# Causal masks added by VectorE, and branch gates projected with group 0's values, in a two-layer decoder on one core

## The chip, the cores and the metric

The kernel runs on one core of a Trainium2 chip. A core has TensorE (PE in the rows, with its weight loads as PEld), VectorE (DVE), ScalarE (ACT), GpSimd (POOL) and SyncE (SP), which issues DMAs here. The metric is the device time of one execution in microseconds, as the median of several runs.

## The reference

A sequence of 512 tokens with 1024 numbers each goes through a retention layer and then through a layer of native sparse attention. Cut to what matters here:

```python
def nsa_shared_kv(h, g_kv, w_kv, ...):          # once, keys and values of all branches
    proj = rmsnorm(h, g_kv) @ w_kv
    k_cmp = compress_blocks(kc, pe_k, w1_k, w2_k)      # gelu(blocks @ w1) @ w2
    v_cmp = compress_blocks(vc, pe_v, w1_v, w2_v)
...
def nsa_layer(h, g_norm, w_in, w_out, ...):
    proj = rmsnorm(h, g_norm) @ w_in
    q, gate, bgate = jnp.split(proj, [q_w, q_w + NSA_W], axis=-1)
    gb = jax.nn.sigmoid(bgate)                         # 16 heads x 3 branches
    ...
    valid_w = kwpos[None, :] <= t[:, None]             # causal
    p_w = jax.nn.softmax(jnp.where(valid_w, s_w, NEG), axis=-1)
    ...
    return gates[..., 0:1] * o_c + gates[..., 1:2] * o_s + gates[..., 2:3] * o_w
```

The two gains (g_kv and g_norm) multiply the same normed rows, so both weights can take their gain first and then share the rows. With 512 tokens all selection blocks fall within the 16 that are kept, so the selected branch is a causal softmax like the window branch.

## The kernel before

All products are made of split operands, a high and a low part: `mm3` (lines 347 to 354) issues three matmuls for each pair of chunks, and line 353 is therefore the line of nearly all of TensorE's work. TensorE holds results in PSUM tiles named d, s, pt and o. Weights come through the class `Stream`: blocks of up to 128 x 1024 numbers are loaded, in the order that `order()` writes out by hand, into four raw slots; GpSimd multiplies a gain into a block (line 169), ScalarE rounds it to its high part (line 187), VectorE makes the low part (line 205, and 203 for the gates' block "bg"); six slots hold finished blocks. A call of `tick` in the code puts the next block's steps into the engines' queues at that point, so the order of the code is the order of each engine.

The second layer begins with `norm_rows` (lines 670 to 674) and transposed rows aH, aL; `v_proj` (704 to 714) makes group 0's values for four tiles of tokens from two blocks "kvv" of 256 columns, and the low parts of these blocks are what its matmuls need. `compress` (766 on) then builds compressed keys (b = 0) and values (b = 1). Its `block(s)` adds and splits a block of tokens on VectorE (lines 774, 776 on ScalarE, 779), and then runs 24 matmuls of 256 columns with the weights "wk" or "wv" into tile o; there are eight such steps, and dense products stand between them: for b = 1 the four query products of group 0 (`q_proj`, 24 matmuls of 512 columns, evacuated in line 727). Beside the last part, the gelu with two transposes (line 800), `bg_proj` makes the branch gates: 16 matmuls of 512 columns (lines 865, 866, 868) with weights of 48 or 96 columns, and later four transposes (line 1024) and three small steps (1026 to 1028) bring them to rows. `k_proj` (745 on) follows.

The attention loop runs over 4 groups and 8 units each, a head times two branches. Beside unit u the scores of unit u + 1 are made: `scores` fills three banks s, for token tile 3, tile 2, and tiles 0 and 1; even units carry 32 more columns of compressed keys. After its three products each bank gets the causal mask, as a matmul of the identity `idb` with the triangle `tri` (0 and -1e30, bf16) that adds into the bank: line 927 for tiles 3 and 2, line 941 for both diagonals of the last bank. VectorE then takes negated maxima (line 951), ScalarE exponentials (952), GpSimd scales (965); line 891 adds the mask of the compressed columns. `probs_T` transposes the probabilities in two parts (line 974), and their split (362 on ScalarE, 363 on VectorE) feeds `values`. Dense products (`fillers`) stand before, between and after the parts.

Of the kernel before, what the change touches and what calls it, by code (L numbers as in the profile page):

```python
# [24 lines left out]
M_TRI, M_CMP, M_ID, M_END = 0, 128, 256, 384  # L25
# [22 lines left out]
def order():  # L48
    """The blocks of [128, 1024] that stream in, in the order in which they are used.

    A block is (array, first row, rows, first column, columns)."""
# [41 lines left out]
    o += [("bg", 0, 1024, 0, 48)] + kk(0)  # L93
# [23 lines left out]
class Stream:  # L117
    """Blocks of weights: loaded into raw slots, then multiplied by their gains and split into
    a high and a low part. Every tick moves each of these steps on by a block."""
# [9 lines left out]
    def first(self, n, i):  # L129
        """Splits one half of a block at the start."""  # L130
# [14 lines left out]
    def tick(self, n=None):  # L145
        """Moves on by up to n blocks, as far as there is room."""
# [14 lines left out]
    def mul(self):  # L161
# [4 lines left out]
        if g is not None and w < 512:  # L166
            r3 = raw.rearrange("p (k n) -> p k n", k=m)
            for k in (slice(0, m // 2), slice(m // 2, m)):
                self.nc.gpsimd.tensor_mul(r3[:, k], r3[:, k],  # L169
                                          g[:, k, None].to_broadcast([128, m // 2, w]))  # L170
        self.nm += 1

    def high(self):
# [8 lines left out]
        if self.order[n][0] == "bg":  # L182
            # The low parts go beside the high ones, 48 columns each.
            self.nc.scalar.activation(hi[:, :2 * m * w].rearrange("p (k n) -> p k n", k=m)[:, :, :w],
                                      raw.rearrange("p (k n) -> p k n", k=m), AF.Copy)
        elif g is None or w < 512:
# [7 lines left out]
    def low(self):  # L194
# [6 lines left out]
        if self.order[n][0] == "bg":  # L201
            h, l = (a[:, :2 * m * w].rearrange("p (k n) -> p k n", k=m) for a in (hi, self.hi[s]))
            self.nc.vector.tensor_sub(l[:, :, w:], raw.rearrange("p (k n) -> p k n", k=m), h[:, :, :w])
        elif g is None or w < 512:
# [32 lines left out]
def decoder(ctx: ExitStack, tc: tile.TileContext, x, xT, stream, cst, msk, gains, fnorm, out):  # L237
# [33 lines left out]
    idb = masks[:, M_ID:M_ID + 128]  # L271
# [7 lines left out]
    def scal(n):  # L279
        """Columns for small per-token numbers, handed out in turn."""  # L280
# [10 lines left out]
    def gain(key):  # L291
        n, r0, nr = key[0], key[1], key[2]
        base = {"kv": G_KV, "kvv": G_KV, "nin": G_NSA, "bg": G_NSA, "pg0": G_PLE,
                "pg1": G_PLE + 8, "rout": G_GN}.get(n)
        if base is None:
            return None
        return gn[:, base + r0 // 128:base + (r0 + nr) // 128]
# [3 lines left out]
    # ---- places of layer 1  # L301
# [15 lines left out]
    # ---- constants and the start of the streams  # L317
# [3 lines left out]
    # The clock of the tensor engine rises while the first loads run.  # L321
# [34 lines left out]
    def wst(p, o, k0=0, k1=NK):  # L356
        """Columns of a block on the partitions, tokens along the free axis."""
# [7 lines left out]
    def rstd(ms, scale):  # L365
        """(ms * scale + EPS) ** -0.5 in place."""
# [7 lines left out]
    def to_aT(t, src, bank="pt"):  # L374
        """Rows of tile t onto the free axis, split."""
# [8 lines left out]
    # ---- layer 1: x^T, its reciprocal rms into the rotary tables  # L384
# [319 lines left out]
    def v_proj(g, t, p, bank="d", tick=True):  # L704
# [7 lines left out]
        if t == 3:  # L712
            p[0].done()
            p[1].done()
# [475 lines left out]
```

## Time and profile before

| | |
|---|---|
| median of 3 runs | 1165.9 us (1163.51 to 1167.29) |
| span of the profiled execution | 1164.6 us |
| busy TensorE / weight loads | 1147.4 / 964.1 us |
| busy VectorE / ScalarE / GpSimd | 697.5 / 486.5 / 299.5 us |
| granted TensorE clock over the span | nine tenths or more in each of 40 slices |

The share of busy time is an average over the whole span. TensorE's row is full, so its rare waits show up in the brackets of a timeline's rows, with the engine and the line that ended them, and they are read stage by stage. Matmuls overlap, so the distance from one start to the next tells what one costs, and the duration beside it does not.

### The profile page before, as it was taken

The numbers are of one execution on the slowest core, as the hardware profiler recorded it, in microseconds if no ns is written. First come the engines' busy times: TensorE is split into PE (matmuls) and PEld (weight loads), VectorE is DVE, ScalarE is ACT, GpSimd is POOL, SyncE is SP. The second block draws the span as 40 slices with busy tenths as digits, with TensorE's granted clock in tenths as the row PEclk, the third lists the DMA queues.
The fourth block names the chain that finished last, engine by engine and source line by source line (L and its number), as shares of the span: only waits on it lengthen the run. The fifth ranks groups of instructions, "written<-read, shape, count | busy, mean of one in ns | idle before, by whom it ended". The sixth has DMA issues, their size and how long they took to land. (4 is left out here: it accounts for less than half of the span.)

```text
span 1164.6 us, 15379 instructions
## 1 busy us (share of the span) xinstructions
PE 1147.4 (99%) x5922; PEld 964.1 (83%) x5922; DVE 697.5 (60%) x1147; ACT 486.5 (42%) x915; POOL 299.5 (26%) x341
## 2 busy tenths in 40 slices
PE   9999999999999999999899999999999999999997
PEld 7888888888888888988687888888898888888886
DVE  4746336544634566578767645767367664677555
ACT  6433233232323455445454433444344443444653
POOL 0212003002100213213654333344153530321012
PEclk9999999999999999999899999999999999999999
DMA  8422321322232131245522112221021211221211
GB/s 330 159 83 74 119 88 55 93 97 73 91 109 84 62 111 54 95 161 158 165 73 91 37 37 72 74 73 55 19 91 55 73 55 47 81 79 49 73 37 73
DMA packets 29593, 101.98 MB, mean 88 GB/s; under 512 B 3536, under 2 KB 3792, under 8 KB 29520
## 3 DMA queue, kind: packets, MB, share of 16 engines
q1 hardware_dynamic: 29088, 100.22, 26.3%
q8 instruction: 46, 0.75, 0.3%
q10 hardware_dynamic: 432, 0.79, 0.2%
q14 instruction: 27, 0.22, 0.1%
HBM read 98.89 MB, written 2.10 MB: 87 GB/s over the span
## 5 line engine op out<-in xcount | busy, mean ns | idle before, releaser
L353 PE MATMUL d<-arenaR 128*128 128x512 f32 (+1 forms) x2904 | 677.9, 386 | 1.8 <-DVE arenaR L205 0.8
L353 PEld LDWEIGHTS d<-arenaR 128*128 128x128 f32 x2904 | 522.5, 188 | 105.0 <-DVE arenaR L205 1.8
L353 PE MATMUL s<-arenaR 128*128 128x512 f32 (+7 forms) x1182 | 246.9, 357 | 0.0
L205 DVE TENSOR_TENSOR arenaR<-arenaF,arenaR 128x1024 fp32r<-128x1024 f32 x141 | 191.2, 1374 | 64.1 <-ACT arenaR L187 63.9
L353 PEld LDWEIGHTS s<-arenaR 128*128 128x128 f32 x1182 | 196.3, 190 | 26.5
L187 ACT ACTIVATE arenaR<-arenaF 128x1024 fp32r<-128x1024 f32 x141 | 145.6, 1052 | 107.9 <-PE s L353 68.4
L169 POOL TENSOR_TENSOR arenaF<-arenaF 128x512 f32<-128x512 f32 (+1 forms) x114 | 146.7, 1309 | 127.4 <-DMA arenaF<-stream_dram 127.4
L353 PE MATMUL o<-arenaR 128*128 128x512 f32 (+2 forms) x744 | 128.7, 323 | 4.5 <-DVE arenaR L779 3.5
L965 POOL TENSOR_SCALAR arenaF<-arenaF 128x512 f32<-128x512 f32 (+3 forms) x128 | 66.8, 542 | 244.6 <-DVE arenaF L962 118.9
L353 PEld LDWEIGHTS o<-arenaR 128*128 128x128 f32 x744 | 114.8, 191 | 17.0 <-DVE arenaR L779 4.1
L363 DVE TENSOR_TENSOR arenaR<-pt,arenaR 128x512 fp32r<-128x512 f32 (+1 forms) x141 | 82.8, 617 | 39.8 <-ACT arenaR L362 38.4
L362 ACT ACTIVATE arenaR<-pt 128x512 fp32r<-128x512 f32 (+1 forms) x141 | 70.7, 540 | 82.5 <-PE pt L974 44.4
L952 ACT ACTIVATE arenaF<-s,arenaF 128x512 f32<-128x512 f32 (+3 forms) x128 | 66.6, 525 | 88.5 <-DVE arenaF L951 87.7
L369 POOL TENSOR_TENSOR arenaF<-arenaF 128x1 f32<-128x1 f32 (+1 forms) x25 | 14.2, 568 | 292.0 <-DVE arenaF L368 292.0
L951 DVE TENSOR_REDUCE arenaF<-s 128x1 f32<-128x512 f32 (+3 forms) x128 | 59.0, 486 | 42.6 <-ACT arenaF L952 28.2
L353 PE MATMUL pt<-arenaR 128*128 128x512 f32 (+1 forms) x384 | 75.9, 349 | 0.0
L353 PEld LDWEIGHTS pt<-arenaR 128*128 128x128 f32 x384 | 62.7, 188 | 9.4
L209 DVE SCALAR_TENSOR_TENSOR arenaR<-arenaF,arenaR 128x512 fp32r<-128x512 f32 x64 | 45.7, 762 | 35.0 <-PE pt L353 21.4
L191 ACT ACTIVATE arenaR<-arenaF 128x512 fp32r<-128x512 f32 x64 | 43.0, 720 | 46.6 <-issue 22.3
L974 PEld LDWEIGHTS pt<-arenaF 128*128 128x128 f32 x318 | 38.5, 140 | 9.7 <-DVE arenaR L363 1.8
L974 PE MATMUL pt<-arenaF 128*128 128x128 f32 x318 | 45.0, 272 | 1.4 <-DVE arenaR L363 1.4
L1013 DVE TENSOR_TENSOR arenaF<-arenaF,d 128x512 f32<-128x512 f32 x64 | 41.8, 682 | 6.9 <-PE d L353 6.6
(138 smaller groups left out, 705.0 us busy)
## 6 DMA issues: line engine op xcount, KB each, us to landing
arenaF<-stream_dram SPq DMA_DIRECT2D x174, 512.0 KB, 3.5
arenaF<-xT_dram SPq DMA_DIRECT2D x8, 256.0 KB, 5.1
arenaF<-x_dram SPq DMA_DIRECT2D x4, 512.0 KB, 7.8
out_dram<-arenaF SPq DMA_DIRECT2D x3, 512.0 KB, 2.6
arenaF<-cst_dram SPq DMA_DIRECT2D x4, 256.0 KB, 3.8
arenaF<-stream_dram ACTq DMA_DIRECT2D x2, 256.0 KB, 4.2
arenaF<-stream_dram SPq DMA_DIRECT2D x2, 256.0 KB, 5.8
arenaF<-cst_dram SPq DMA_DIRECT2D x1, 512.0 KB, 9.5
```

The source lines that it names most:

```text
L169: self.nc.gpsimd.tensor_mul(r3[:, k], r3[:, k], g[:, k, None].to_broadcast([128, m // 2, w]))
L187: self.nc.scalar.activation(hi[:, :m * w], raw, AF.Copy)
L191: self.nc.scalar.activation(hi[:, c], raw[:, c], AF.Copy, scale=g[:, k:k + 1])
L205: self.nc.vector.tensor_sub(lo[:, :m * w], raw, hi[:, :m * w])
L209: self.nc.vector.scalar_tensor_tensor(lo[:, c], raw[:, c], g[:, k:k + 1], hi[:, c], op0=OP.mult, op1=OP.subtract)
L353: pe.matmul(o, a, b, start=start and i == 0, stop=stop and i == n - 1)
L362: act.activation(h, src, AF.Copy)
L363: dve.tensor_sub(l, src, h.bitcast(F32))
L951: dve.reduce_max(mx[:, i:i + 1], w, axis=mybir.AxisListType.X, negate=True)
L952: act.activation(Pu[:, PO[i]:PO[i] + n], w, AF.Exp, bias=mx[:, i:i + 1], accum_out=sm_[:, i:i + 1])
L965: pool.tensor_scalar(w, w, sm_[:, i:i + 1], 1.0, op0=OP.mult, op1=OP.mult)
L974: pe.transpose(p[:, f:f + 128], Pu[:, PO[i] + 128 * j:PO[i] + 128 * j + 128], ident)
```

## The change

The change has three parts. In `scores` the mask matmuls go, and VectorE adds the same triangle to the bank in place, ahead of its maxima: one add of 128 columns for tiles 3 and 2 each, one of 2 x 128 for the last bank. The identity `idb` is no longer loaded. Second, the 48 columns of branch gates join group 0's value weights as three blocks "kvb" of 384, 384 and 256 rows and 304 columns; GpSimd multiplies the two gains into the two sorts of columns; `v_proj(0, t)` makes 304 columns instead of 256 and ScalarE takes tanh of the last 48; `bg_proj`, its block and its transposes go. Third, the steps 6 and 7 of the value compression follow steps 4 and 5 at once, and the last query product takes the place of `bg_proj` beside the gelu.

```diff
 def order():
-    o += vv(0) + [("kv", 0, 1024, 128 * g, 128) for g in range(4)]
+    o += [("kvb", r, min(384, 1024 - r), 0, 304) for r in (0, 384, 768)]
+    o += [("kv", 0, 1024, 128 * g, 128) for g in range(4)]
     for n, dense in (("wk", [("kv", 0, 1024, 512 + 128 * g, 128) for g in range(4)]),
-                     ("wv", q(0))):
+                     ("wv", q(0)[:3])):
...
-    o += [("bg", 0, 1024, 0, 48)] + kk(0)
+    o += [("wv", 512 * i, 512, 0, 256) for i in (6, 7)] + [q(0)[3]] + kk(0)
...
     def mul(self):
+            if self.order[n][0] == "kvb":
+                for c, g in ((slice(0, 256), g[0]), (slice(256, 304), g[1])):
+                    self.nc.gpsimd.tensor_mul(r3[:, :, c], r3[:, :, c], g[:, :, None]
+                                              .to_broadcast([128, m, c.stop - c.start]))
...
     def v_proj(g, t, p, bank="d", tick=True):
-        o = psum(bank)[:, :256]
-        for a in range(2):
-            mm3(o, [(aH[:, t, 4 * a + k], aL[:, t, 4 * a + k], p[a].h[:, k], p[a].l[:, k])
-                    for k in range(4)], a == 0, a == 1)
-        split_psum(v2H[:, t], v2L[:, t], o)
+        n = 256 if g else 304
+        o = psum(bank)[:, :n]
+        k0 = 0
+        for q in p:
+            m = q.h.shape[1]
+            mm3(o, [(aH[:, t, k0 + k], aL[:, t, k0 + k], q.h[:, k], q.l[:, k])
+                    for k in range(m)], k0 == 0, k0 + m == NK)
+            k0 += m
+        split_psum(v2H[:, t], v2L[:, t], o[:, :256])
+        if g == 0:
+            act.activation(bg[:, t], o[:, 256:], AF.Tanh, scale=0.5)
...
-    for h in range(4):
+    for h in range(3):
         f = q_proj(0, h)
...
-    f = bg_proj()
-    act.activation(small[:, 250:251], half, AF.Exp)
-    next(f)
+    next(comp1)
+    next(comp1)
+    f = q_proj(0, 3)
+    next(f)
+    act.activation(small[:, 250:251], half, AF.Exp)
     next(comp1)
     run(f)
...
-            mm3(w, [(q2H[h][:, c], q2L[h][:, c], k2H[b][:, lo:hi], k2L[b][:, lo:hi])], first, hi == 32)
-            if i > 1 and hi > 32:
-                pe.matmul(w[:, hi - lo - 128:], idb, tri, start=False, stop=True)
+            mm3(w, [(q2H[h][:, c], q2L[h][:, c], k2H[b][:, lo:hi], k2L[b][:, lo:hi])], True, True)
...
-            if i == 1:
-                both = bass.AP(tensor=o.tensor, offset=o.offset + e,
-                               ap=[list(o.ap[0]), [256 + e, 2], [1, 128]])
-                pe.matmul(both, idb, tri[:, None, :].to_broadcast([128, 2, 128]), start=False,
-                          stop=True)
...
+            if 1 in bank:
+                d = bass.AP(tensor=o.tensor, offset=o.offset + e,
+                            ap=[list(o.ap[0]), [256 + e, 2], [1, 128]])
+                dve.tensor_add(d, d, tri[:, None, :].to_broadcast([128, 2, 128]))
+            else:
+                d = o[:, at[0] + 128 * bank[0]:][:, :128]
+                dve.tensor_add(d, d, tri)
...
-    p = psum("pt")
-    for t in range(NT):
-        pe.transpose(p[:, 96 * t:96 * t + 96], bgT[:96, 128 * t:128 * t + 128], ident[:96, :96])
-    p4 = p[:, :384].rearrange("p (t a n) -> p t a n", t=NT, a=2)
-    act.activation(bg, p4[:, :, 0], AF.Copy)
-    dve.tensor_add(bg, bg, p4[:, :, 1])
-    act.activation(bg, bg, AF.Tanh, scale=0.5)
     dve.tensor_scalar(bg, bg, 0.5, 0.5, op0=OP.mult, op1=OP.add)
```

The new file has other line numbers: `mm3`'s matmul is line 355, the split of a product 365, the blocks' add and split 783 and 788, the gelu's transposes 809, the query's evacuation 736, the mask adds 937 and 940, the maxima 944. The rows below give a line, the operation, the tile written (with its number), the tile read and the size.

At the end of the compression, TensorE's row before. Tile o_3724 is the compressed value's sum, each x24 two steps of it; d_3836 and d_3910 are the third and fourth query product, d_3976 the gates:

```order
L353 MATMUL d_3836<-arenaR_64 128x512 x24
L353 MATMUL o_3724<-arenaR_64 128x256 x24
L353 MATMUL d_3910<-arenaR_64 128x512 x24
L353 MATMUL o_3724<-arenaR_64 128x256 x24
L866 MATMUL d_3976<-arenaR_64 96x512
L868 MATMUL d_3976<-arenaR_64 48x512
```

And after, with the sum in o_3733, the fourth query product in d_3954 and k_proj in d_3990:

```order
L355 MATMUL d_3845<-arenaR_64 128x512 x24
L355 MATMUL o_3733<-arenaR_64 128x256 x48
L355 MATMUL d_3954<-arenaR_64 128x512 x12
L809 MATMUL pt_3968<-arenaF_63 128x128 x2
L355 MATMUL d_3954<-arenaR_64 128x512 x12
L355 MATMUL d_3990<-arenaR_64 128x512 x24
```

The last four steps of the sum now stand together, and the fourth query product stands behind them, in two halves around the transposes.

VectorE at the same place before, from the third query's evacuation to the fourth's:

```order
L727 SCALAR_TENSOR_TENSOR arenaR_64<-d_3836,arenaR_64 128x512
L205 TENSOR_TENSOR arenaR_64<-arenaF_63,arenaR_64 128x1024 x2
L774 TENSOR_TENSOR arenaF_63<-arenaF_63 128x16x31
L779 TENSOR_TENSOR arenaR_64<-arenaF_63,arenaR_64 128x512
L774 TENSOR_TENSOR arenaF_63<-arenaF_63 128x16x31
L205 TENSOR_TENSOR arenaR_64<-arenaF_63,arenaR_64 128x1024
L203 TENSOR_TENSOR arenaR_64<-arenaF_63,arenaR_64 128x8x48
L779 TENSOR_TENSOR arenaR_64<-arenaF_63,arenaR_64 128x512
L727 SCALAR_TENSOR_TENSOR arenaR_64<-d_3910,arenaR_64 128x512
```

And after:

```order
L736 SCALAR_TENSOR_TENSOR arenaR_64<-d_3845,arenaR_64 128x512
L205 TENSOR_TENSOR arenaR_64<-arenaF_63,arenaR_64 128x1024 x2
L783 TENSOR_TENSOR arenaF_63<-arenaF_63 128x16x31
L788 TENSOR_TENSOR arenaR_64<-arenaF_63,arenaR_64 128x512
L783 TENSOR_TENSOR arenaF_63<-arenaF_63 128x16x31
L205 TENSOR_TENSOR arenaR_64<-arenaF_63,arenaR_64 128x1024 x2
L788 TENSOR_TENSOR arenaR_64<-arenaF_63,arenaR_64 128x512
L205 TENSOR_TENSOR arenaR_64<-arenaF_63,arenaR_64 128x1024 x2
```

The two splits of blocks keep their places; ahead of the last one there stands a whole block's low part where the gates' one stood.

VectorE at the first value product before, from the last tile's norm to the first value tile's split (d_3156):

```order
L672 TENSOR_SCALAR arenaF_63<-arenaF_63 128x512
L205 TENSOR_TENSOR arenaR_64<-arenaF_63,arenaR_64 128x1024
L363 TENSOR_TENSOR arenaR_64<-d_3156,arenaR_64 128x256
L363 TENSOR_TENSOR arenaR_64<-o_3183,arenaR_64 128x256
L363 TENSOR_TENSOR arenaR_64<-pt_3210,arenaR_64 128x512
```

And after (first value tile d_3159):

```order
L674 TENSOR_SCALAR arenaF_63<-arenaF_63 128x512
L205 TENSOR_TENSOR arenaR_64<-arenaF_63,arenaR_64 128x608
L205 TENSOR_TENSOR arenaR_64<-arenaF_63,arenaR_64 128x1024
L365 TENSOR_TENSOR arenaR_64<-d_3159,arenaR_64 128x256
L365 TENSOR_TENSOR arenaR_64<-o_3187,arenaR_64 128x256
```

The low part of 608 columns (the third piece, 2 x 304) has come in between the norm and the low part that stood there.

## Rows read from the trace of the kernel before

**Rows 1.** page: an engine (busy us, share, instructions); a group of instructions

```profile
PE 1147.4 (99%) x5922; PEld 964.1 (83%) x5922; DVE 697.5 (60%) x1147; ACT 486.5 (42%) x915; POOL 299.5 (26%) x341
...
L205 DVE TENSOR_TENSOR arenaR<-arenaF,arenaR 128x1024 fp32r<-128x1024 f32 x141 | 191.2, 1374 | 64.1 <-ACT arenaR L187 63.9
```

**Rows 2.** groups by line and form: busy us, mean ns | idle before

```profile
L927 PE MATMUL s<-masks 128*128 128x128 bf16 x64 | 14.7, 230 | 0.0
L941 PE MATMUL s<-masks 128*128 128x256 bf16 x32 | 9.1, 283 | 0.0
```

**Rows 3.** timeline of TensorE, even unit's scores: start, us, work

```profile
768.99 0.81 PE L353 MATMUL s<-arenaR 128*128 128x416 f32 x3
769.64 0.23 PE L927 MATMUL s<-masks 128*128 128x128 bf16 x1
...
770.83 0.28 PE L941 MATMUL s<-masks 128*128 128x256 bf16 x1
770.87 3.00 PE L353 MATMUL d<-arenaR 128*128 128x512 f32 x12
773.71 1.03 PE L974 MATMUL pt<-arenaF 128*128 128x128 f32 x8
```

**Rows 4.** timeline of TensorE, plain run of 512-column products and what follows

```profile
479.52 27.39 PE L353 MATMUL d<-arenaR 128*128 128x512 f32 x120
506.75 3.04 PE L353 MATMUL o<-arenaR 128*128 128x256 f32 x24
```

**Rows 5.** timeline of all engines, first value product of group 0

```profile
467.05 3.12 PE L353 MATMUL d<-arenaR 128*128 128x256 f32 x24
...
470.00 3.05 PE L353 MATMUL o<-arenaR 128*128 128x256 f32 x24
...
471.13 0.58 DVE L672 TENSOR_SCALAR arenaF<-arenaF 128x512 f32<-128x512 f32 x1
471.64 2.06 DVE L205 TENSOR_TENSOR arenaR<-arenaF,arenaR 128x1024 fp32r<-128x1024 f32 x1
```

**Rows 6.** timeline of TensorE, end of the compression

```profile
562.80 0.63 PE L353 MATMUL d<-arenaR 128*128 128x512 f32 x2
...
571.64 0.39 PE L353 MATMUL o<-arenaR 128*128 128x256 f32 x1 [0.60 <-DVE arenaR L205]
574.39 2.50 PE L353 MATMUL o<-arenaR 128*128 128x256 f32 x10 [2.37 <-DVE arenaR L779]
576.69 0.63 PE L866 MATMUL d<-arenaR 128*96 128x512 f32 x1
...
582.18 1.07 PE L353 MATMUL d<-arenaR 128*128 128x512 f32 x4
```

**Rows 7.** timeline of VectorE, the same stretch

```profile
567.25 0.69 DVE L779 TENSOR_TENSOR arenaR<-arenaF,arenaR 128x512 fp32r<-128x512 f32 x1 [0.70 <-ACT arenaR L776]
...
571.50 1.39 DVE L203 TENSOR_TENSOR arenaR<-arenaF,arenaR 128x384 fp32r<-128x384 f32 x1
572.82 1.52 DVE L779 TENSOR_TENSOR arenaR<-arenaF,arenaR 128x512 fp32r<-128x512 f32 x1
```

**Rows 8.** groups by line and form, VectorE, reads of score banks

```profile
L951 DVE TENSOR_REDUCE arenaF<-s 128x1 f32<-128x256 f32 x32 | 13.6, 425 | 28.2 <-ACT arenaF L952 28.2
...
L891 DVE TENSOR_TENSOR arenaF<-s,masks 128x64 f32<-128x64 f32 x32 | 7.1, 222 | 7.8 <-ACT arenaF L952 7.6
```

**Rows 9.** timelines: ordinary unit (split, transposes), then two tight units

```profile
775.42 1.28 DVE L363 TENSOR_TENSOR arenaR<-pt,arenaR 128x512 fp32r<-128x512 f32 x2
...
777.36 0.38 PE L974 MATMUL pt<-arenaF 128*128 128x128 f32 x2
...
632.04 0.44 PE L974 MATMUL pt<-arenaF 128*128 128x128 f32 x2 [1.37 <-DVE arenaR L363]
...
1053.76 1.67 PE L353 MATMUL d<-arenaR 128*128 128x512 f32 x6 [0.32 <-DVE arenaF L740]
```

**Rows 10.** busy us of five engines in a stretch, PEclk, DMA

```profile
575.00:580.00 5.00, 5.00 (x17) 3.54 (x17) 3.05 (x2) 1.40 (x2) 4.84 (x4) 0.50 0.73 215
```

More of the change, by code (lines that the diff above doesn't have):

```diff
@@ L167, in mul @@
             r3 = raw.rearrange("p (k n) -> p k n", k=m)
-            for k in (slice(0, m // 2), slice(m // 2, m)):
-                self.nc.gpsimd.tensor_mul(r3[:, k], r3[:, k],
-                                          g[:, k, None].to_broadcast([128, m // 2, w]))
+            if self.order[n][0] == "kvb":
[3 more added lines that the diff above has]
+            else:
+                for k in (slice(0, m // 2), slice(m // 2, m)):
+                    self.nc.gpsimd.tensor_mul(r3[:, k], r3[:, k],
+                                              g[:, k, None].to_broadcast([128, m // 2, w]))
         self.nm += 1
@@ L181, in high @@
         hi = self.hi[s]
[L182 to L186, printed above, removed]
+        if g is None or w < 512:
             self.nc.scalar.activation(hi[:, :m * w], raw, AF.Copy)
@@ L200, in low @@
         hi, lo = self.hi[s].bitcast(F32), self.lo[s]
[L201 to L204, printed above, removed]
+        if g is None or w < 512:
             self.nc.vector.tensor_sub(lo[:, :m * w], raw, hi[:, :m * w])
@@ L270, in decoder @@
     fb += 700
-    idb = masks[:, M_ID:M_ID + 128]
     def psum(tag, shape=None):
@@ L712, in v_proj @@
         if t == 3:
-            p[0].done()
-            p[1].done()
+            for q in p:
+                q.done()
     def v_pieces(g):
+        if g == 0:
+            return [W.get("kvb", r, min(384, 1024 - r), 0, 304) for r in (0, 384, 768)]
         return [W.get("kvv", 512 * a, 512, 256 * g, 256) for a in (0, 1)]
@@ L856, in decoder @@
         next(comp1)
-    def bg_proj():
-        p = W.get("bg", 0, 1024, 0, 48)
-        o = psum("d")
-        w = W.hi[p.s][:, :768].rearrange("p (k n) -> p k n", k=NK)
-        for k in range(NK):
-            if k:
-                pe.matmul(o[:48], w[:, k, :48], aL[:, :, k], start=False, stop=False)
-            pe.matmul(o[:96], w[:, k], aH[:, :, k], start=k == 0, stop=k == NK - 1)
-            if k == 0:
-                pe.matmul(o[:48], w[:, k, :48], aL[:, :, k], start=False, stop=False)
-            if k == 3:
-                yield
-        act.activation(bgT[:96], o[:96], AF.Copy)
-        W.tick()
-        p.done()
-        yield
-    f = bg_proj()
+    next(comp1)
+    next(comp1)
+    f = q_proj(0, 3)
+    next(f)
     act.activation(small[:, 250:251], half, AF.Exp)
-    next(f)
     next(comp1)
@@ L921, in scores, with block @@
         cmp = []
-        def block(w, i, lo, hi, first=True):
+        def block(w, i, lo, hi):
             c = slice(128 * i, 128 * i + 128)
-            mm3(w, [(q2H[h][:, c], q2L[h][:, c], k2H[b][:, lo:hi], k2L[b][:, lo:hi])], first, hi == 32)
-            if i > 1 and hi > 32:
-                pe.matmul(w[:, hi - lo - 128:], idb, tri, start=False, stop=True)
+            mm3(w, [(q2H[h][:, c], q2L[h][:, c], k2H[b][:, lo:hi], k2L[b][:, lo:hi])], True, True)
         for bank in ((3,), (2,), (0, 1)):
@@ L934, in scores @@
                 n = 128 * i + 128 + e - lo
[L935 removed]
+                block(o[:, f:f + n], i, lo, lo + n)
                 at.append(f + e - lo)
                 f += n
[L938 to L942 removed]
             if e and 2 in bank:
```

18 lines of the change are left out of this document (9 added, 9 removed).

## The prediction

> **What bounds the kernel now.** I read the page first. TensorE is busy for 1147.4 of 1164.6 us [rows 1]: it is the bound nearly everywhere, so a part of the change is worth what it takes off TensorE's row, less what it makes TensorE wait. The groups of instructions by line and form give the number of mask matmuls and how long they are shown busy [rows 2], but that is not their price, because matmuls overlap. The price is in the starts of neighbours in the timeline [rows 3, 4]. Then I read the three places where TensorE waits for VectorE or nearly does: the first value product [rows 5], the end of the compression [rows 6, 7], and the probabilities' transposes in the attention [rows 8, 9]. The reader should see there that VectorE, with 60% busy over the whole span, is a chain with little room in just the stretches to which the change adds work.
>
> **The masks on TensorE.** There are 64 of 128 columns and 32 of 256 [rows 2]. Plain spacing, from start to start, is (506.75 - 479.52) / 120 = 0.227 us at 512 columns [rows 4] and (470.00 - 467.05) / 24 = 0.123 at 256 [rows 5]; in between, 416 columns give 0.188. In one even unit [rows 3] the last mask starts at 770.83 and the next product at 770.87: a mask takes a slot of 0.04 us. The three products of 416 columns behind the first mask take 769.64 - 768.99 = 0.65 where 3 x 0.188 = 0.56 is plain: 0.09 more. The 12 products behind the third take 773.71 - 770.87 = 2.84 where 12 x 0.227 = 2.72 is plain: 0.12 more. Behind the second, a run of small products, I see nothing extra. So a unit pays 3 x 0.04 + 0.09 + 0.12 = 0.33, and 32 units pay 10.6; with reading error I take 0.32 a unit, **-10.2 us**. The ends are the slots alone, 96 x 0.04 = 3.8, and the whole busy time, 14.7 + 9.1 = 23.8.
>
> The Trainium skill, TensorE: Matmul & The Clock Gate, section Back-to-back issue gap, gives a matmul at full clock N / 2.4 + 2.5 ns to the next one, 56 ns for 128 columns and 109 for 256. By it the masks would be worth an estimated 64 x 0.056 + 32 x 0.109 = 7.1 us, and the whole sum would come out 3.1 us later than mine. The trace differs from the rule at both ends: the slot is 0.04 us, and part of the cost shows only on the product behind it.
>
> **The branch gates on TensorE.** Four transposes go; eight of 128 columns take 1.03 us in the row [rows 3], so **-0.5**. The added 48 columns sit in 4 tiles x 8 chunks x 3 = 96 value matmuls; by the slope between the two spacings, (0.227 - 0.123) / 256 = 0.00041 us a column, that is 96 x 48 x 0.00041, **+1.9** (between 0, if the columns hide in an instruction's floor, and 96 x 0.123 x 48/256 = 2.2). The 16 gate matmuls run from 576.69 to 582.18, 5.5 us [rows 6], with two transposes among them (0.2); 16 x 0.227 = 3.6 of it is plain, and 1.65 is a half clock. What they free is decided below, because another product takes their place. Four tanh of 48 columns come onto ScalarE behind the value product's high parts; nothing waits for them before the attention, 15 us and more of TensorE's work later, so they cost nothing, and 0.2 each if that cover were gone. The number of streamed blocks stays the same, so SP's queue and GpSimd's gain products have one block for another.
>
> **The first value product waits for its third piece.** Before, TensorE starts it at 467.05 and VectorE has both pieces' low parts ready; the low part behind the fourth tile's norm on VectorE (471.13, then 471.64 with 2.06 us) belongs to the next weights [rows 5]. After, as the order shows, that place is the third piece's, 608 columns. TensorE reaches it after two pieces, 18 matmuls of 304 columns at 0.123 + 48 x 0.00041 = 0.143: 467.05 + 2.57 = 469.6. The low part cannot start before about 471.64 and takes 608/1024 of 2.06 = 1.2, or, at the mean of all blocks (1.37, [rows 1]), 0.8: ready at 472.4 to 472.9. A wait of 2.8 to 3.3: **+3.1**. Nothing lies behind it on TensorE's queue that could fill it. The lower end is 0, should VectorE get to the piece before TensorE. After the waits of 0.60 and 2.37 us at 571 to 574 [rows 6] the granted clock was at 0.50 for all of 575 to 580 [rows 10], that is the 1.2 GHz level; the gate matmuls there paid 1.65 us and the 10 before them 576.69 - 574.39 - 10 x 0.123 = 1.07, together 2.7. This new wait may or may not do the same; I take half, **+1.3**, with ends of 0 and 2.7.
>
> **The end of the compression.** Before, TensorE has wv 4, 5 behind it at 562.80, then runs the last query product (24 matmuls, 5.45 us), and even so it waits for the operands of wv 6, 7: 0.60 at 571.64 for a low part and 2.37 at 574.39 for the last block's split [rows 6]. VectorE splits the last two blocks at 567.25 and 572.82, the second right behind a low part of the gates' weights (1.39) [rows 7]. After, wv 6, 7 come at 562.8 with nothing ahead of them, but VectorE's list is the same length: a 1024-column low part stands where the gates' 384-column one stood, so the last split is at about 572.8 to 573.4 again and is ready near 574.4. TensorE simply waits longer, some 5 us at the first split. Then 10 matmuls are left as before to about 576.7, and in place of the gates' 3.6 us stand the query's 5.45 + 0.2 and a half clock that costs 1.65 as before, or up to 2.5 behind the longer wait: the next product (k_proj) starts at 576.7 + 7.3 to 8.15 = 584.0 to 584.85, against 582.18. The gates' 5.5 us are thus taken off a stretch that VectorE bounds: **+1.8**, from -4 (the split comes as early as TensorE, and the query product runs at full clock) to +4 (both low parts ahead take 2 us as at 471.64).
>
> **The masks on VectorE.** The nearest rows are the compressed mask's add from PSUM, 0.222 us for 64 columns, and a maximum over 256 columns, 0.425 [rows 8]: on the line between them 0.29 for 128 and 0.42 for 256, 1.0 a unit and 32 us in all. An add waits for the same product as its maximum did, so behind it on VectorE stands what stood behind the maximum, only later. In an ordinary unit TensorE's second transposes start at 777.36 while the split that they need, the first of two of 1.28 together, ends at about 776.1 [rows 9]: 1.3 us of room. The maximum over 256 columns, the last of a unit, comes after 28.2 us of idle time in 32 units, 0.88 each, ended by ScalarE's exponentials [rows 8]: the later adds go into that time, and the chain gets longer by the first (0.29) and at times by a second (0.6), not by all three. An ordinary unit hides it. Six units have under 0.6 us of room, four early in group 0 and two near the end; TensorE waits for VectorE in two of them already, 1.37 us at 632.04 and 0.32 at 1053.76 [rows 9]. There the 0.32 saved on TensorE only makes it wait earlier, and the longer chain comes on top: 5 x 0.32 + 5 x 0.45 - 0.4 of room = **+3.5**, from 0 to 7.9 (6 x (1.0 + 0.32)).
>
> **The sum.** -10.2 - 0.5 + 1.9 + 3.1 + 1.3 + 1.8 + 3.5 = +0.9. The span 1164.6 becomes 1165.5; the median of the runs is 1.3 above the profiled span, so 1166.8: no difference that a measurement of this kernel can tell, which I put at 0.3%, 3.5 us.
>
> **The rivals.**
> **Room everywhere** (faster). VectorE hides the adds in the six units too (0 in place of 3.5), the clock holds behind the new wait (0 for 1.3), and the last split comes 1 us earlier, since the low parts ahead of it run at their mean (0.8 for 1.8): 0.9 - 5.8 = -4.9, **1161**. For it: the 0.88 us that VectorE idles before the last maximum. Against: the waits in [rows 9] name VectorE.
> **The maxima's chain becomes VectorE's own** (slower). If VectorE rather than ScalarE paces the reductions, a tight unit gets longer by all three adds: 7.9 in place of 3.5, +4.4, **1171**. Place: the tight units of group 0 and the last two heads. It decides from the point where the adds take more than the 0.88 us of idle time; they take 1.0, and in a tight unit a low part of 1.4 to 2 us may fall between them.
> **The masks cost TensorE only their slots.** Then the change does not do what it is made for: 3.8 in place of 10.2, +6.4, **1173**. For it: behind the second mask nothing extra shows. Against: the two products behind the first and third.
> The page's rule on the issue gap lies between this rival and my sum, at an estimated 1170; its chance is in this rival's.
>
> **How the numbers follow.** Forecast 0.42 (1163 to 1169, all within 0.3%), room everywhere 0.25 (1156 to 1162, faster), VectorE's chain 0.23 (1169.5 to 1174, slower), slots alone 0.10 (slower). So faster 0.25, same 0.42, slower 0.33. The range reaches from 1158.5, which leaves out about a third of the first rival, to 1173.5, which leaves out about half of the last and some of the chain: 1 in 10 on each side. It takes in the compression's -4 and the tight units' +4.3 taken one at a time.
>
> **What will show it.** In the trace after: no matmul on masks, and 416-column products behind one another at 0.19; adds of 0.29 and 0.42 us on VectorE; a wait of about 3 us of TensorE near 469.6 for the low part; a wait of about 5 us for wv 6 and k_proj's start 1 to 3 us later relative to the value stage; in group 2, units 0.3 us shorter each; at the six tight units a longer wait for the split. It is wrong if the third piece is ready in time, if k_proj starts 3 us earlier than I say, or if ordinary units begin to wait too.

## The result, and the profile after

The changed kernel is slower: 1172.0 us (1171.3 to 1176.5) against 1165.5 before, a ratio of 1.0062 with an interval of 1.0041 to 1.0083. In a second set of runs, on another occasion, it took 1174.7 us, ratio 1.0080 (1.0067 to 1.0094). The forecast said 1166.8 and no difference; the range, 1158.5 to 1173.5, held the first time, the forecast of no difference was wrong. That the range held is partly luck: the second set's median lies 1.2 us above it.

The page of after (engines with busy time, share and instructions; then groups with busy time, mean ns, and the idle time ahead of them with what ended it), as in [rows 1]:

```profile
PE 1140.1 (97%) x5806; PEld 970.0 (83%) x5806; DVE 727.8 (62%) x1242; ACT 490.8 (42%) x916; POOL 294.9 (25%) x341
...
L355 PE MATMUL d<-arenaR 128*128 128x512 f32 (+2 forms) x2904 | 678.1, 386 | 10.4 <-DVE arenaF L1006 3.6
...
L355 PE MATMUL o<-arenaR 128*128 128x512 f32 (+3 forms) x744 | 133.4, 331 | 11.0 <-DVE arenaR L788 5.0
...
L967 PE MATMUL pt<-arenaF 128*128 128x128 f32 x318 | 45.1, 273 | 3.2 <-DVE arenaR L365 3.2
```

TensorE has less work, 1140.1 us busy for 1147.4, and VectorE 30 us more, as forecast. But the third column has grown: TensorE idles 10.4 us before products into d, 11.0 before products into o and 3.2 before the transposes, where it was 1.8, 4.5 and 1.4 on the page of before, and each time VectorE ends the largest part of it.

To see where the time went I cut the span at seven starts on TensorE that every kernel has: the first value product of group 0; the first 512-column product behind the value products; the first product of k_proj; the first transposes of the probabilities of unit 0, of unit 6, of unit 27 and of unit 31 (the 32 units are counted through); and the end. What lies ahead of the first cut is nearly the same program in all kernels and varied from one profiled execution to the next by up to 3.3 us, so it is left out; the first profile of after has 2.0 us of its 1174.7 there, all within the first 21 us, where TensorE waits 1.92 us for ScalarE and the granted clock was 0.89 and 0.77 from 5 to 15. That execution was the slowest of its four (1176.5 us); the others, at 1171.3 to 1172.6, have no profile.

| stage, us in before | after | masks only | gates only | cover | no masks | hybrid | tick late | best | query back |
|---|---|---|---|---|---|---|---|---|---|
| value products 12.47 | +7.04 | +0.01 | +7.05 | +3.01 | 0.00 | 0.00 | +3.01 | 0.00 | +5.52 |
| to k_proj 102.66 | +2.20 | -0.99 | +1.69 | +1.35 | -0.93 | -0.18 | -3.81 | -3.74 | -2.95 |
| to unit 0 21.63 | -0.73 | -0.76 | -0.20 | -0.74 | -0.72 | 0.00 | -0.37 | +0.82 | +0.76 |
| units 0 to 6 79.26 | +2.35 | +3.20 | -0.32 | +1.63 | +1.20 | -0.34 | +2.32 | -0.35 | +1.66 |
| units 6 to 27 358.85 | -4.51 | -4.36 | -0.34 | -4.53 | -8.14 | -4.84 | -4.54 | -4.98 | -4.27 |
| units 27 to 31 44.36 | +1.71 | +1.67 | +0.02 | +1.69 | -0.03 | -0.02 | +1.72 | +0.02 | +1.71 |
| to the end 78.35 | -0.01 | -0.01 | +0.01 | +0.02 | +0.04 | -0.02 | +0.02 | +0.05 | -0.01 |

The column of after adds up to +8.1: 9.2 in the first two stages, and only -1.2 in the attention, where 10 us of mask matmuls were taken out. The other columns are the experiments below. How far one profile of a stage can be trusted shows in its second row: masks only, no masks, the hybrid and the kernel with later compressed steps run the program of before up to k_proj, and yet come out at -0.99, -0.93, -0.18 and +0.28. Masks only and no masks had a granted clock of 0.66 and 0.75 from 575 to 580, before and the other two 0.50 to 0.54.

**The first value product** in the timeline of after (start, us, engine, line, work, idle before), to be held against [rows 5]:

```profile
469.05 2.91 PE L355 MATMUL d<-arenaR 128*128 128x304 f32 x19
...
473.13 0.58 DVE L674 TENSOR_SCALAR arenaF<-arenaF 128x512 f32<-128x512 f32 x1
...
475.30 0.96 PE L355 MATMUL d<-arenaR 128*128 128x304 f32 x5 [3.35 <-DVE arenaR L205]
476.10 5.04 PE L355 MATMUL o<-arenaR 128*128 128x304 f32 x24
480.98 1.04 PE L382 MATMUL pt<-arenaF 128*128 128x128 f32 x8
481.77 3.60 PE L355 MATMUL d<-arenaR 128*128 128x304 f32 x24
485.21 3.52 PE L355 MATMUL s<-arenaR 128*128 128x304 f32 x24
```

The wait stands where it was forecast, for the low part behind the last tile's norm, and took 3.35. The tile behind it needs 480.98 - 476.10 = 4.88 us for 24 products, the tile after that 485.21 - 481.77 = 3.44: the clock was at its lower level, 1.2 GHz for 2.4, for part of the stretch. The windows of after (busy us of five engines, granted clock, DMA share, GB/s), as in [rows 10]:

```profile
475.00:480.00 5.00, 4.70 (x22) 4.70 (x23) 1.81 (x3) 0.66 (x3) 0.95 (x1) 0.66 0.62 188
480.00:485.00 5.00, 5.00 (x39) 5.00 (x39) 1.71 (x3) 1.58 (x4) 3.12 (x4) 1.00 0.05 21
```

**The end of the compression**, TensorE and VectorE of after, against [rows 6, 7]:

```profile
568.53 3.03 PE L355 MATMUL o<-arenaR 128*128 128x256 f32 x24
576.31 0.79 PE L355 MATMUL o<-arenaR 128*128 128x256 f32 x2 [4.75 <-ACT arenaR L785]
577.90 3.15 PE L355 MATMUL o<-arenaR 128*128 128x256 f32 x12 [0.80 <-DVE arenaR L788]
584.11 2.50 PE L355 MATMUL o<-arenaR 128*128 128x256 f32 x10 [3.06 <-DVE arenaR L788]
586.41 4.22 PE L355 MATMUL d<-arenaR 128*128 128x512 f32 x12
...
579.46 3.99 DVE L205 TENSOR_TENSOR arenaR<-arenaF,arenaR 128x1024 fp32r<-128x1024 f32 x2
583.38 0.68 DVE L788 TENSOR_TENSOR arenaR<-arenaF,arenaR 128x512 fp32r<-128x512 f32 x1
```

TensorE waits 4.75, 0.80 and 3.06 us in place of 0.60 and 2.37 (and of 0.79 within the query product, at 564.22, which [rows 6] leaves out); the last block's split (583.38) stands behind two low parts that take 3.99 together. The 12 products from 586.41 take 4.06 to the next start, 0.34 each, again at the lower clock. Before had the lower clock here too: its page shows nine tenths or more in 39 slices and eight tenths in the one from 553 to 582 us, not in all 40.

**The attention**: what TensorE waited for, with the total, the times and the longest. First before, then after, from k_proj's end to the last unit:

```profile
PE pt L974 <- DVE arenaR L363: 1.4, 1, 1.4
PE pt L910 <- POOL arenaF L965: 0.6, 3, 0.3
...
```

```profile
PE d L355 <- DVE arenaF L1006: 3.4, 7, 0.9
PE pt L967 <- DVE arenaR L365: 3.2, 3, 1.8
PE d L355 <- DVE arenaF L749: 1.3, 1, 1.3
PE o L355 <- DVE arenaR L365: 0.8, 1, 0.8
...
```

All of the waits in these two lists, the lines left out too, add up to 2.7 us before and 10.1 after. The seven at the top were not in the forecast at all: TensorE waits for line 1006, the sum over heads (1013 before), which frees a bank d. Five of them, 0.41 us each, lie in ordinary units (9, 13, 17, 21 and 25), the others in units 5 and 29. One of them in an ordinary unit of after, and the same place of before:

```profile
755.92 0.42 DVE L944 TENSOR_REDUCE arenaF<-s 128x1 f32<-128x256 f32 x1 [0.58 <-ACT arenaF L945]
...
757.05 1.03 PE L967 MATMUL pt<-arenaF 128*128 128x128 f32 x8
...
757.55 0.29 DVE L886 TENSOR_TENSOR arenaF<-arenaF 128x128 f32<-128x128 f32 x1
...
757.76 1.28 DVE L1006 TENSOR_TENSOR arenaF<-arenaF,d 128x512 f32<-128x512 f32 x2
758.50 3.02 PE L355 MATMUL d<-arenaR 128*128 128x512 f32 x12 [0.41 <-DVE arenaF L1006]
```

```profile
745.31 0.29 DVE L894 TENSOR_TENSOR arenaF<-arenaF 128x128 f32<-128x128 f32 x1
745.42 1.04 PE L974 MATMUL pt<-arenaF 128*128 128x128 f32 x8
745.52 1.28 DVE L1013 TENSOR_TENSOR arenaF<-arenaF,d 128x512 f32<-128x512 f32 x2
746.26 3.04 PE L353 MATMUL d<-arenaR 128*128 128x512 f32 x12
```

The sums stand on VectorE behind the whole chain of maxima and behind the compressed branch's steps. Before, they start 0.10 us after the transposes on TensorE start (745.52, 745.42) and the first ends just as the bank is wanted. After, they start 0.71 later than the transposes (757.76, 757.05), and TensorE waits.

The clock has a part in the attention too, which the forecast left out. Behind the longest wait of after, in unit 2, and behind a wait of the same length at the same place of the cover kernel (below):

```profile
643.09 0.44 PE L967 MATMUL pt<-arenaF 128*128 128x128 f32 x2 [1.80 <-DVE arenaR L365]
644.48 3.41 PE L355 MATMUL o<-arenaR 128*128 128x512 f32 x12
```

```profile
635.51 0.44 PE L974 MATMUL pt<-arenaF 128*128 128x128 f32 x2 [1.79 <-DVE arenaR L365]
636.57 2.18 PE L355 MATMUL o<-arenaR 128*128 128x512 f32 x12
```

In after the granted clock was 0.88 and 0.78 from 640 to 650, and the 12 products took 3.24 us to the next start; in cover it stayed at 1.00, and they took 2.02. So 1.2 of the +2.35 from unit 0 to 6 is the clock's. Masks only and no masks have such a fall in this stage as well, about 1.5 us each; cover, the query product back and the hybrid have none.

### The profile page after: what moved, and what is told of

Its sections match the earlier page's. It is cut to its first block, busy times and chain, and to the rows that moved or that the text cites. A ratio compares the mean times of both kernels' runs of the same rounds, so it can differ in the third digit from the quotient of the medians.

```text
span 1174.7 us, 15278 instructions
## 1 busy us (share of the span) xinstructions
PE 1140.1 (97%) x5806; PEld 970.0 (83%) x5806; DVE 727.8 (62%) x1242; ACT 490.8 (42%) x916; POOL 294.9 (25%) x341
## 5 line engine op out<-in xcount | busy, mean ns | idle before, releaser
L355 PE MATMUL d<-arenaR 128*128 128x512 f32 (+2 forms) x2904 | 678.1, 386 | 10.4 <-DVE arenaF L1006 3.6
L355 PE MATMUL s<-arenaR 128*128 128x512 f32 (+8 forms) x1182 | 239.5, 353 | 0.2 <-DVE arenaR L829 0.2
L205 DVE TENSOR_TENSOR arenaR<-arenaF,arenaR 128x1024 fp32r<-128x1024 f32 (+1 forms) x142 | 194.1, 1386 | 66.1 <-ACT arenaR L190 66.0
L355 PEld LDWEIGHTS s<-arenaR 128*128 128x128 f32 x1182 | 200.3, 188 | 29.8 <-DVE arenaR L829 0.3
L190 ACT ACTIVATE arenaR<-arenaF 128x1024 fp32r<-128x1024 f32 (+1 forms) x142 | 145.8, 1048 | 104.4 <-PE s L355 68.4
L176 POOL TENSOR_TENSOR arenaF<-arenaF 128x512 f32<-128x512 f32 x108 | 137.0, 1291 | 126.2 <-DMA arenaF<-stream_dram 126.1
L355 PE MATMUL o<-arenaR 128*128 128x512 f32 (+3 forms) x744 | 133.4, 331 | 11.0 <-DVE arenaR L788 5.0
L355 PEld LDWEIGHTS o<-arenaR 128*128 128x128 f32 x744 | 119.1, 198 | 24.0 <-DVE arenaR L788 5.8
L944 DVE TENSOR_REDUCE arenaF<-s 128x1 f32<-128x512 f32 (+3 forms) x128 | 62.9, 491 | 22.2 <-ACT arenaF L945 18.9
```

Source lines behind the costliest of these rows:

```text
L176: self.nc.gpsimd.tensor_mul(r3[:, k], r3[:, k], g[:, k, None].to_broadcast([128, m // 2, w]))
L190: self.nc.scalar.activation(hi[:, :m * w], raw, AF.Copy)
L205: self.nc.vector.tensor_sub(lo[:, :m * w], raw, hi[:, :m * w])
L355: pe.matmul(o, a, b, start=start and i == 0, stop=stop and i == n - 1)
L944: dve.reduce_max(mx[:, i:i + 1], w, axis=mybir.AxisListType.X, negate=True)
```

## The experiments

All ratios are against the kernel before, in the same set of runs. Of the twelve expectations below, the hybrid's and the second combination's ranges hold the result; splits ahead came 1.0 us under its range, eight came 0.2 to 1.7 above theirs, and the third combination 4.1.

**Masks only.** The diff's part in `scores`, alone, on the kernel before.

> The kernel before with the masks moved to VectorE and nothing else changed. Theory (TensorE saves about 10 us, and the longer chain of maxima gives nearly all of it back as waits for VectorE in the units with little room and for the banks of the output products): 1163 to 1166 us, about -1, with some 9 us of new waits in the attention. Rival (VectorE has room, all of the loss is the gates' part): 1155 to 1157. Second rival (the mask matmuls cost TensorE only their slots of 0.04 us): 1170 or more.

1166.2 us, ratio 1.0008 (0.9998 to 1.0017): no difference. **Gates only** is the reverse, the changed kernel with the mask matmuls put back:

> The changed kernel with the masks back as matmuls; the gates' columns beside the values and the new order of the last query product stay. Theory (a wait of 3.3 us and a half clock in the first value product, 1.9 us of columns, 2.6 us at the end of the compression, 0.4 us of transposes saved): 1171 to 1174 us, +6 to +8. Rival (the gates' part is about neutral and the loss is VectorE's in the attention): 1165 to 1167.

1174.9 us, ratio 1.0083 (1.0070 to 1.0097). So all of the loss is the gates' part, and the masks' part gives back what it saves. The waits that the masks' part brings to the attention, in the masks-only kernel, are those of after:

```profile
PE pt L975 <- DVE arenaR L363: 4.1, 3, 1.9
PE d L353 <- DVE arenaF L1014: 3.3, 7, 0.8
PE d L353 <- DVE arenaF L740: 1.3, 1, 1.3
```

**No masks.** The masks-only kernel without its adds:

```diff
-                dve.tensor_add(d, d, tri[:, None, :].to_broadcast([128, 2, 128]))
+                pass
...
-                dve.tensor_add(d, d, tri)
+                pass
```

> The kernel before with the causal masks left out altogether: neither matmuls nor adds (scores of later tokens stay in, so it computes another softmax). It shows what the mask matmuls cost TensorE. Theory (0.32 us a unit, less what the tight units of group 0 already wait): 9 to 10 us less than before, 1155 to 1157, and none of the waits for the output products' banks. Rival (slots of 0.04 us alone): 4 us less, 1161.

1157.6 us, ratio 0.9929 (0.9917 to 0.9942), 7.6 less than before: less than the 9 to 10 that I expected, and twice the rival's 4. From unit 6 to 27, where there is room, it gains 8.14 in 21 units, 0.39 each. The scores of an even unit, 15 products, take 768.25 - 765.92 = 2.33 here; before, the same products start at 768.25 and the next one at 770.87 [rows 3], 2.62, and the 12 products behind them take 2.77 for 2.84:

```profile
765.92 2.50 PE L353 MATMUL s<-arenaR 128*128 128x512 f32 x15
768.25 2.93 PE L353 MATMUL d<-arenaR 128*128 128x512 f32 x12
```

In the tight units it gains nothing: -0.03 from 27 to 31, where TensorE only comes earlier to the same wait, without any add on VectorE. More than the +1.20 from unit 0 to 6 is the clock's: behind a wait of 2.13 us it was 0.71 from 630 to 635, and 12 products took 3.51 us for 2.01 in before; without these 1.5 us the stage would be at an estimated -0.3. In the profiled execution that fall is most of what is missing to the 9 us. Beside masks only, whose profile has a fall of the same size, the adds themselves cost 2.0 + 3.8 + 1.7 = 7.5 in the three stages of the units.

**Hybrid.** VectorE's adds in 15 units with room, mask matmuls in the other 17:

```diff
+        idx = 8 * g + u
+        dv = 7 <= idx <= 26 and idx % 4 != 2
...
-            if i > 1 and hi > 32:
+            if not dv and i > 1 and hi > 32:
...
+            if dv and 1 in bank:
...
+                dve.tensor_add(d, d, tri[:, None, :].to_broadcast([128, 2, 128]))
+            elif dv:
```

> The kernel before with VectorE's adds only in 15 of the 32 units: numbers 7 to 26, without every fourth (10, 14, 18, 22, 26), where the moved masks made TensorE wait 0.57 us for a bank; mask matmuls in the other 17. Theory (an ordinary unit has room for the adds, a tight one has none): the 15 units keep their 0.32 us and no new wait shows, 4.5 to 5.5 us less than before, 1160 to 1161. Rival (every add on VectorE is paid somewhere): 1164 to 1166.

1160.7 us, ratio 0.9956 (0.9943 to 0.9968), and its longest wait in the attention is the one that before had:

```profile
PE pt L985 <- DVE arenaR L363: 1.4, 1, 1.4
PE pt L910 <- POOL arenaF L976: 0.6, 3, 0.2
PE o L353 <- DVE arenaR L363: 0.4, 1, 0.4
```

15 units bring 4.84 us, 0.32 each. An ordinary unit does hide the adds; every fourth unit and the tight ones do not.

**Compressed steps later.** Adds in all of units 7 to 26, with two steps moved:

```diff
+        yield
         mx, sm_ = scal(4), scal(4)
         dve.reduce_max(mx, q, axis=mybir.AxisListType.X)
         dve.tensor_sub(q, q, mx[:, :, None].to_broadcast([128, 4, 32]))
-        yield
```

> As the last one, but with adds in all of units 7 to 26, and with two VectorE steps of the compressed branch (the maximum over 32 columns and its subtraction, 0.6 us) moved behind the sums over heads that free the banks. Theory (those sums wait behind the chain of maxima, so 0.6 us less ahead of them takes the wait of 0.57 us away at units 10, 14, 18, 22, 26): 6 to 7 us less than before, 1158.5 to 1159.5. Rival (the moved steps are late for the compressed probabilities, or the wait stays): 1161 to 1164.

1161.0 us, ratio 0.9952 (0.9938 to 0.9966). In its trace no wait for a sum over heads is left ahead of the last unit: the five waits were VectorE's order, as the theory has it. But units 6 to 27 gain only 5.28, for 4.84 in the hybrid, and 27 to 31 lose 1.04; there neither kernel has an add, and the hybrid loses nothing (-0.02), so it is the moved steps that cost it. The hoped for 1 to 2 us on top of the hybrid did not come.

**Cover.** In the changed kernel the first two pieces of two value tiles run before the third piece of either:

```diff
-    v_proj(0, 0, p, "d", False)
-    v_proj(0, 1, p, "o", False)
+    o2 = [psum(b)[:, :304] for b in ("d", "o")]
+    for t in (0, 1):
+        v_part(0, t, p, o2[t], (0, 1))
+    for t in (0, 1):
+        v_proj(0, t, p, None, False, o2[t], (2,))
```

> The changed kernel with the first two pieces of value tiles 0 and 1 run one after the other before the third piece of either: 18 more matmuls, 2.6 us, stand ahead of the wait for the third piece's low part. Theory: the wait falls from 3.4 to about 1 us and the clock stays at its upper level, so 3 to 4 us less than the changed kernel, 1168 to 1169. Rival (what is gained there is waited for again at the end of the compression, which VectorE bounds): within 1 us of the changed kernel, 1171 to 1173.

1170.2 us, ratio 1.0036 (1.0023 to 1.0050), 4.4 less than the changed kernel in the same set. The wait falls to 0.84 and the clock stays at 1.00 in both windows from 470 to 480:

```profile
471.50 0.30 PE L355 MATMUL d<-arenaR 128*128 128x304 f32 x1
472.64 0.96 PE L355 MATMUL d<-arenaR 128*128 128x304 f32 x5 [0.84 <-DVE arenaR L205]
```

The stage is +3.01 now, of which about 1.0 is the wait, so the columns cost 2.0.

**The changed kernel again**, for its second profile:

> The changed kernel once more, for a second profile, since its first profiled execution was 4 to 5 us above the other runs. Theory: the same waits at the same places (3.4 us in the first value product, 5 and 3 us in the compression, 0.6 us at every fourth unit of the attention); what was more in the first profile is 2 us before the first product. Rival: waits of the first profile are missing here, and a story that rests on them falls. Both: 1171 to 1173 us.

1174.7 us. Every wait stands again where it was (3.35 in the value product; 4.80, 0.82 and 3.06 in the compression; 3.4, 3.2 and 1.3 in the attention). The value products took 20.43 for 19.51, since the lower clock lasted longer.

**Splits ahead of low parts** (tick late). On the cover kernel, the last two blocks' splits no longer wait behind low parts of the stream:

```diff
+            late = b and s > 5
-            if s > 1:
+            if s > 1 and not late:
                 W.tick()
             dve.tensor_sub(bkL[s % 4], blk[s % 2], bkH[s % 4].bitcast(F32))
+            if late:
+                W.tick()
```

> The cover kernel (changed kernel with the first value product's wait mostly covered), with the last two blocks' splits of the value compression put ahead of the low parts of streamed weights on VectorE instead of behind them. Theory (the wait of 3.4 us for the last block is VectorE working on low parts of 2 us each that nobody needs yet): 2 to 4 us less than the cover kernel, 1166 to 1168. Rival (the low parts are late instead, for the query product or k_proj): 1170, as the cover kernel.

1165.0 us, ratio 0.9998 (0.9989 to 1.0006), 5 less than the cover kernel in the other set, more than I expected. The wait for the last block is gone: all 24 products of steps 6 and 7 run through. The lower clock is not gone but shorter:

```profile
564.82 3.03 PE L355 MATMUL o<-arenaR 128*128 128x256 f32 x24
572.55 5.66 PE L355 MATMUL o<-arenaR 128*128 128x256 f32 x24 [4.71 <-ACT arenaR L789]
578.05 2.98 PE L355 MATMUL d<-arenaR 128*128 128x512 f32 x12
```

```profile
570.00:575.00 5.00, 2.42 (x9) 2.12 (x10) 4.30 (x4) 1.58 (x2) 4.20 (x4) 0.53 0.45 165
```

The granted clock is 0.53 from 570 to 575 and 0.79 from 575 to 580, and the 24 products take 5.50 us to the next start, 0.229 each where 0.123 is plain [rows 5]; the 12 products of the query behind them are back at 2.82, for 4.06 in after. The wait of 4.71 us for the first of the two remains; it is the query product that no longer covers it.

**The query product back** in its old place, in the changed kernel, with nothing beside the gelu:

```diff
-                     ("wv", q(0)[:3])):
+                     ("wv", q(0))):
...
-    for h in range(3):
+    for h in range(4):
...
-    next(comp1)
-    next(comp1)
-    f = q_proj(0, 3)
-    next(f)
     act.activation(small[:, 250:251], half, AF.Exp)
     next(comp1)
-    run(f)
```

> The changed kernel with the last query product back between the steps 4, 5 and 6, 7 of the value compression, and nothing beside the gelu. Theory (the moved query product no longer covers the wait for the blocks' splits, and that is why the gates' 5.5 us do not come off): the stretch to k_proj gets 4 to 6 us shorter than in the changed kernel, with a wait of about 1 us for the gelu: 1167 to 1170. Rival (VectorE's list bounds that stretch wherever the query product stands): 1172 to 1175, as the changed kernel.

1170.4 us, ratio 1.0044 (1.0032 to 1.0057), 4.3 less than the changed kernel's 1174.7 in its second set and 1.6 less than its 1172.0 in the first. The stretch to k_proj is 2.95 shorter than before, 5.2 shorter than in after, and the gelu makes TensorE wait 0.47 us; 1.5 of this is given back on the way to unit 0 (+0.76 for -0.73). So the third part of the change, the moved query product, costs 3.7 us up to unit 0, and a part of the gates' product could have come off without it. This profile has one thing more: the wait for the third value piece is the same as in after, yet the clock stayed at 1.00 behind it, and the value products took +5.52 instead of +7.04.

```profile
473.38 0.96 PE L355 MATMUL d<-arenaR 128*128 128x304 f32 x5 [3.36 <-DVE arenaR L205]
```

The half clock there is worth 1.5.

**Combinations.** The hybrid's masks on three arrangements: the gates as before with the splits ahead; the gates beside the values, covered, with the splits ahead; and that with the query product back.

> The hybrid kernel (gates as before, VectorE's adds in 15 ordinary units) with the last two blocks' splits of the value compression ahead of the streamed low parts. Theory (the wait of 3.4 us there and the half clock behind it, 2.7, go): 4 to 5 us less than the hybrid, 1155.5 to 1157. Rival (the low parts are waited for instead): 1160 to 1161.

> The tick_late kernel (gates beside the values, first wait mostly covered, splits ahead of low parts) with VectorE's adds only in the hybrid's 15 units and mask matmuls in the rest. Theory: the attention's waits go and it comes out 4 us below tick_late, 1160.5 to 1161.5. Rival (the changed attention waits hide lateness of the stream from the stages before): 1163 or more.

> As best_after, with the last query product back in its place before steps 6 and 7, and nothing beside the gelu. Theory (with the splits early the stretch is TensorE's, so the gates' 5.5 us come off, less about 1 us of wait for the gelu; the first value product keeps its 3 us): 1157 to 1159. Rival (the gelu's chain is longer than 3 us uncovered): 1160 to 1162.

They took 1158.4 us, ratio 0.9943 (0.9930 to 0.9957); 1161.2, ratio 0.9966 (0.9953 to 0.9978); and 1163.1, ratio 0.9983 (0.9974 to 0.9992). The first is the best of all and beats both kernels, though it is only 2.3 us below the hybrid, where I expected 4 to 5. The second, 3.9 below splits ahead, came out as its theory says. The first one's trace shows that the split came early and something else was late:

```profile
570.49 0.71 DVE L780 TENSOR_TENSOR arenaR<-arenaF,arenaR 128x512 fp32r<-128x512 f32 x1 [0.70 <-ACT arenaR L776]
571.12 2.06 DVE L205 TENSOR_TENSOR arenaR<-arenaF,arenaR 128x1024 fp32r<-128x1024 f32 x1
```

```profile
573.23 1.58 PE L353 MATMUL o<-arenaR 128*128 128x256 f32 x11 [2.29 <-DVE arenaR L205]
```

The last split ends at 571.2, but the low part of the last weights now stands behind it, and TensorE waits 2.29 us for that one. What is gained is the other wait and the clock, which stayed at 1.00 from 570 to 585; 0.8 of the 3.7 us are given back on the way to unit 0. The third arrangement lost behind k_proj's start what it won before it (-5.19 to k_proj, +6.23 to unit 0). It is slower, as the rival says, and still 1 us above the rival's range; and its reason is not the rival's, for TensorE waits only 0.70 us for the gelu. With nothing but k_proj between gelu and scores, it waits 0.73 and 0.82 for the splits there, and the scores behind them run at half clock:

```profile
587.33 0.44 PE L356 MATMUL s<-arenaR 128*128 128x128 f32 x2 [0.73 <-ACT arenaR L365]
588.59 5.93 PE L356 MATMUL s<-arenaR 128*128 128x128 f32 x25 [0.82 <-DVE arenaR L366]
```

```profile
590.00:595.00 5.00, 5.00 (x21) 4.37 (x21) 3.59 (x5) 0.59 (x1) 1.37 (x1) 0.50 0.55 163
```

## Why the forecast missed

**The mask matmuls (-10.2).** Right in kind, a little small: 0.39 us a unit where there is room, not 0.32. The Trainium skill's formula for the issue gap (TensorE: Matmul & The Clock Gate, Back-to-back issue gap), by which the masks would have been worth an estimated 0.22 a unit, is too low here; the no-masks kernel decides it. The section itself calls this the isolated gap, which falls short when few columns stream; the prediction left that out. The four transposes, put at -0.5 by a duration, are worth 0.29 by the starts (590.25 to 590.54 in before); gates only gains 0.20 on the way to unit 0.

**The columns (+1.9) and the wait for the third piece (+3.1, clock +1.3).** Right for the first two: 2.0, and 3.35 to 3.5. The clock's +1.3 was half of a fall; it cost 1.5 in one profile of the changed kernel, 2.4 in the other, and nothing in the one with the query product back. The stage came out at +7.0 for a forecast of +6.3. The low part of 608 columns took 1.62 us where I had 0.8 to 1.2; GpSimd multiplied a gain into the next block at the time.

**The end of the compression (+1.8).** The size is right, +2.2, in a stage that can move by 1 us by itself, and TensorE waits for VectorE's list as described. The reason why the gates' 5.5 us don't come off is right only in part: it was the move of the query product that did this, and not VectorE's bound alone. Back in its place, the stretch was 5.2 us shorter, 3.7 up to unit 0.

**The attention's waits (+3.5).** This is the step that failed. In after the three stages of the units and the one ahead of them gave -1.2; with the forecast's terms they should have given -10.2 - 0.5 + 3.5 = -7.2. These 6 us are nearly all of the 7.2 between the forecast's sum, +0.9, and the stages' +8.1. Of the +3.5, 1.6 is saving lost in tight units and 1.9 the adds' own price; masks only beside no masks puts that price at 7.5. Three things were missed in it. First, "an ordinary unit hides it", which put 3.8 us at nothing, was checked against one wait only, that of the second transposes for the split [rows 9], where there was room of 1.3 us. The sums over heads stand on VectorE behind the same chain, and they free the banks d; there the room was some 0.1 us in every fourth unit. That is the 3.4 us of line 1006, 2.1 of it in ordinary units. Second, near the end not two units were tight but three: from unit 27 on the stretches from one unit to the next lose 0.57, 0.61 and 0.53, and the fourth nothing (+1.71), where without adds they are even (-0.03). Third, the sum has no term for the clock in the attention, and behind the longer wait of unit 2 it cost 1.2 in after. (In the prediction's last reckoning of the range, the tight units' +4.3 should be the +4.4 of its rival; nothing hangs on it.)

**The rivals.** "Room everywhere" fell: masks only shows the waits. "The maxima's chain becomes VectorE's own" named the right engine and the right sign and 1171, but put the price into the tight units, where only half of it was; of the 7.5 us that the adds cost, 3.8 lie in ordinary units. "Slots alone" fell with no masks: 7.6 us for its 4.

**The gates' part as a whole.** In gates only, the first two stages are +8.7, forecast +8.1. Both parts of the forecast for it held; the loss was in plain view, and only the masks' gain was counted too high against it.

## What to carry to other kernels

When work is added to an engine's chain, list everything that stands behind the chain on that engine, and for each the engine that waits for it; the room of the nearest waiter says nothing about the next. A gain on the bounding engine is worth its full size only in the stages where that engine is the bound; a change that can be switched on stage by stage, as the hybrid does, keeps the gain and leaves the waits. Before a product is moved, ask what wait it was covering: here two short reorders were worth several us each: the query product 3.7 up to unit 0, the splits ahead of the low parts 2.3 in one kernel and about 5 in another.

## What the runs showed of the hardware

The same pause lowers TensorE's clock in one execution and not in another. Behind the wait of 3.35 us for the third value piece, the clock fell in after (0.66 from 475 to 480 us) and in the second profile of it (0.50), and stayed at 1.00 in the kernel with the query product back, with a wait of 3.36 in the same place. Behind 1.80 us in unit 2 it fell in after and behind 1.79 it stayed in cover. Behind 2.29 us in the best kernel (the first combination) it stayed at 1.00; in the hybrid, behind two waits at the same place, it was 0.54 from 575 to 580. A forecast can price such a fall, 1.5 and 2.4 us in the value products here, but it should carry it as a chance.

A low part of 1024 columns takes VectorE 1.22 us alone (1.21 to 1.23 in the 91 of after that meet no gain product of GpSimd's) and 1.2 to 2.2 while GpSimd multiplies gains (23 that lie wholly or nearly so beside such products, median 1.6): two took 3.99 at 579.46 in after, where GpSimd worked from 576.26 to 582.4. The two are seen side by side; no run takes the gain products away. Where low parts stand ahead of something urgent, 2 us each is the number to use.
